# Gate and up products of SwiGLU feature tiles 4 to 7 by Strassen's seven products, with sums of input blocks and the residual parked in DRAM

## The chip, the cores and the metric

The kernel runs as one program on one core of a Trainium2 chip. The metric is the device time of one execution in microseconds (us), lower is better; the time of a kernel is the median of its runs. The result must agree with the reference in float32.

## The reference

A hybrid decoder trunk of two layers on 512 tokens of width 1024. Each layer is a half-step SwiGLU, a mixing of three kinds of attention, and a second half-step SwiGLU, each with an RMSNorm in front and behind. What the change touches is the SwiGLU, which runs four times:

```python
D_MODEL = 1024; SEQ = 512; DEPTH = 2
D_FF = ((8 * D_MODEL // 3 + 127) // 128) * 128        # 2816, 22 tiles of 128

def _swiglu(t, w_gate, w_up, w_down):
    return (jax.nn.silu(t @ w_gate) * (t @ w_up)) @ w_down
...
    h = x
    for l in range(DEPTH):
        f = _swiglu(_rmsnorm(h, ffn1_pre_g[l]), ffn1_w_gate[l], ffn1_w_up[l], ffn1_w_down[l])
        h = h + 0.5 * _rmsnorm(f, ffn1_post_g[l])
        u = _rmsnorm(h, mix_pre_g[l])
        ...                                           # three attentions of u, gated and merged
        h = h + _rmsnorm(merged @ w_out[l], mix_post_g[l])
        f = _swiglu(_rmsnorm(h, ffn2_pre_g[l]), ffn2_w_gate[l], ffn2_w_up[l], ffn2_w_down[l])
        h = h + 0.5 * _rmsnorm(f, ffn2_post_g[l])
    return h
```

All of it is float32. The names of tiles in the profile end in the sub-layer: a0 and c0 for the two SwiGLUs of layer 0, a1 and c1 for those of layer 1 (the views drop the digit, so that `pga` is a gate product of a0 or a1).

## The kernel before

**A float32 product is three matmuls.** Each operand is kept as a high and a low part, both in the type fp32r; `mm3` (L180 to L184) multiplies high by high, high by low and low by high into one PSUM bank. A split into the parts is a cast on ScalarE (L162) and a subtraction on VectorE (L163). The activations of a sub-layer lie transposed in two tiles `src.us`, each with four blocks of 128 of the model width by 512 tokens in two parts.

**Weights** come in units (class `Unit`, L209). A unit is fetched by one transfer of 512 KB, issued on SyncE (SP), into a ring "raw" of two buffers, and loaded by the split into the rings "wh" and "wl" of four buffers each (`BUFS`, L102). In the plain form a unit holds four blocks of 128 of the inner dimension by 256 columns, 128x1024 as the profile writes it.

**The order.** A queue `Q` (class `Queue`) holds jobs: a list of units and a generator that emits the matmuls. Before a job's matmuls the units of the next jobs are loaded until `AHEAD` = 4 units are ahead, and `fetch_ahead` fills the raw ring whenever a unit has given its buffer back. `weave` puts chains of other work (norms, attention, the end of a sub-layer) between the matmuls of the jobs by an estimate of PE time. When the program is built, a scheduler sets the order of each engine's queue out of this; on the chip each queue runs in order.

**One SwiGLU** (`ffn`, L548) goes through its 22 feature tiles in pairs. The first pair is a `halved` job: its matmuls are 256 tokens wide, so that it can start when half of the tokens are normalised. Each further pair has two plain jobs, `gates` and `ups`, of 48 matmuls each: 2 tiles x 8 blocks of the model width x 3, each 128x512 out of a 128x128 weight block. `hidden` takes Silu of the gate bank on ScalarE (L561) and multiplies by the up bank on VectorE (L566), for the first 16 tiles into the kept tiles `hr` in the rings "k" and "tri".

**The down projection** of the first 16 feature tiles goes in two chunks of 8 (`FC` = 8, `NC` = 2), and each chunk already by Strassen's seven products (`products`, `product`, L656): its first factor is a sum of blocks of `hr` (`first_factor`, L605, which splits it too), its second a sum of blocks of the down weights (class `BlockUnit`, L252), and the product is added into one of three pairs of PSUM accumulators. For every half of the inner blocks a `BlockUnit` keeps two weight blocks in tiles `bt`, which are fetched once and combined in place from product to product (L299 and the lines around it); products 3 and 4 fetch nothing into the raw ring:

```python
BLOCKS = ((0, 0), (1, 0), (0, 0), None, None, (0, 1), (1, 0))
```

Of a finished chunk one product follows after each further plain job. The last 6 feature tiles go through the plain `down` (L705), whose end is interleaved with the residual step, the norm and the transposition of each block of tokens into the next sub-layer's input (class `Sub`: `residual`, `normed`, `turned`).

**PSUM** has two rings of four banks: "mm" for gate and up products, "z" for the accumulators of the down products. **SBUF**: the residual stream `hT`, four tiles of 512 KB, stays in four of the eight buffers of the ring "o" through a SwiGLU. The mixing writes it to a DRAM tensor `hsave` at its start, uses the buffers for other things, and reads it back at its end.

Of the kernel before, what the change touches and what calls it, by code (L numbers as in the profile page):

```python
# [17 lines left out]
P = 128  # L18
# [4 lines left out]
def kernel(  # L23
# [50 lines left out]
    NF = 22  # L74
    FC = 8
    NC = 2
    TRI = (0, 512, 896, 1152)
    TRIW = 1280
    QLO = (0, 128, 256, 256)
# [24 lines left out]
    def stile(shape, tag, name, dt=F32R):  # L104
        return sb.tile(shape, dt, tag=tag, bufs=BUFS[tag], name=name)
# [4 lines left out]
    def pbank(tag, name):  # L110
        return ps.tile([P, S], F32, tag=tag, bufs=4, name=name)
# [97 lines left out]
    class Unit:  # L209
# [8 lines left out]

            return self.raw is None and self.h is None

        def ring(self):

            return True

        def fetch(self):
            if not self.waits():
# [25 lines left out]
    class BlockUnit(Unit):  # L252
# [13 lines left out]
        def waits(self):  # L266
            return not self.fetched

        def ring(self):
            return self.BLOCKS[self.n] is not None  # L270

        def block(self, dst, b):
            r = (b[0] * self.rows + self.k0) * P
# [3 lines left out]
        def fetch(self):  # L277
            if self.fetched:
                return
            self.fetched = True  # L280
            if self.n == 2:
                self.block(self.keep.get(0, self.k0), (0, 1))
            if self.n == 3:
                self.block(self.keep.get(1, self.k0), (1, 1))
            if self.ring():
                Q.fetched += 1
                self.raw = stile([P, self.nk, self.ncol], "raw", "raw_" + self.name, F32)
                self.block(self.raw[:], self.BLOCKS[self.n])

        def load(self):  # L290
            if self.h is not None:
                return
            self.fetch()
            t = self.keep.get(0, self.k0) if self.n >= 2 else None
            b = self.keep.get(1, self.k0) if self.n >= 3 else None
            if self.n < 2:
                src = self.raw[:]
            elif self.n == 2:
                nc.vector.tensor_tensor(t, t, self.raw[:], ALU.subtract)  # L299
                src = t  # L300
            elif self.n == 3:
                nc.vector.tensor_tensor(t, b, t, ALU.subtract)
                src = t
            elif self.n == 4:
                src = b
            elif self.n == 5:
                nc.vector.tensor_tensor(b, b, self.raw[:], ALU.subtract)
                src = b
            else:
                nc.vector.tensor_tensor(t, t, self.raw[:], ALU.subtract)  # L310
                src = t
            self.split_from(src)
            if self.ring():
                self.raw = None
                Q.fetched -= 1
            Q.fetch_ahead()

    class Keep:
# [14 lines left out]
    class Queue:  # L333
# [127 lines left out]
    class Sub:  # L461
# [54 lines left out]
        def normed(self, t):  # L516
# [31 lines left out]
    def ffn(l, src, wg, wu, wd, dst, name, spare, aside=None):  # L548
# [47 lines left out]
        def down_out(t, hf, pt):  # L596
# [5 lines left out]
            nc.vector.tensor_tensor(s[:], f, pt[:], ALU.add)  # L602
            return s[:]

        def first_factor(ci, n):  # L605
# [49 lines left out]

        def products(ci):  # L656

            def make(i, k0):

                if ci == 0:  # L660
                    return stile([P, 2, S], "qo"[i], f"bt{name}_{i}_{k0}", F32)[:]
                if k0 == 0:
                    st["bt", i] = stile([P, 2, 2, S], "k", f"bt{name}_{i}", F32)
                return st["bt", i][:, k0 // 2]
# [6 lines left out]
        marks, todo = {}, iter(())  # L671
        for f in range(0, NF, 2):
            ug = wpair(wg[l], ND, f * P, f"g{name}_{f}")
            uu = wpair(wu[l], ND, f * P, f"u{name}_{f}")
            if f == 0:
                marks["early"] = ug + uu
                for un, place in zip(ug + uu, ("tri", "tri", (spare, spare), (spare, spare))):
                    un.tags = place
                Q.add(ug + uu, lambda ug=ug, uu=uu: halved(0, ug, uu, 0), src.ready((0, 1)))
                Q.add([], lambda ug=ug, uu=uu: halved(0, ug, uu, 1), src.ready(range(NT)))  # L680
                marks["first"] = len(Q.jobs)
                continue
            ci = f // FC if f % FC == FC - 2 and f < NC * FC else None
            Q.add(ug, lambda f=f, ug=ug: gates(f, ug))
            for one in todo:
                Q.add(*one)
                break
            if ci is not None:
                Q.add([], lambda ci=ci: iter(first_factor(ci, 0) or ()))
            Q.add(uu, lambda f=f, uu=uu: ups(f, uu))  # L690
            if ci is not None:
                todo = products(ci)
            for one in todo:
                Q.add(*one)
                break
            if f == FC - 2 and name == "a0":
                Q.add([], vectors)
        if aside is not None:
            Q.add([], aside)
        f0 = NC * FC  # L700
# [322 lines left out]
    def mixing(l, src, ks, vs, dst):  # L1023
# [95 lines left out]
        def reload():  # L1119
            dst.begin()  # L1120
            new_h(f"m{l}")
            for i in range(NT):
                nc.sync.dma_start(hT[i][:], hsave[i])
# [62 lines left out]
    def begin():  # L1186

        sub = subs[0]
        new_h("x")
        Q.hold = True  # L1190
        nc.sync.dma_start(hT[0][:], x[0, 0:P, :])
        sub.gains()
        nc.sync.dma_start(hT[1][:], x[0, P:2 * P, :])
        Q.fetch_ahead()
        for t in range(2, NT):
            nc.sync.dma_start(hT[t][:], x[0, t * P:(t + 1) * P, :])
        sub.begin()
        for t in range(2):
            sub.squared(hT[t][:], sub.sh[t], 0, sub.fs[t][:])
            sub.normed(t)  # L1200
        for t in range(2):
            sub.turned(t)
            Q.jobs[0][0][t].load()
        for t in range(2, NT):
            sub.squared(hT[t][:], sub.sh[t], 0, sub.fs[t][:])
            yield ("wait", 2.0)
            sub.normed(t)
            yield ("wait", 3.0)
            sub.turned(t)
            yield ("pe", 0.9)  # L1210
# [49 lines left out]
```

## Time and profile before

| | |
|---|---|
| Time, median of 3 runs | 2494.75 us (2494.07 to 2495.52) |
| Profiled execution, its time | 2493.26 us |
| Its span | 2491.5 us |
| Mean granted TensorE clock | 0.997 |
| PE busy | 2449.6 us in 12178 recorded matmuls |
| VectorE (DVE) busy | 1541.3 us |
| ScalarE (ACT) busy | 1146.2 us |
| DMA | 270.54 MB, 109 GB/s on average |

The span runs from the first to the last event that the profiler recorded, so the execution's own time is a little longer. The page's rows read: line, engine, operation, tile written <- tiles read, shape, count, then busy time and mean duration in ns, then the idle time of the engine before these instructions and what ended it. PE is TensorE's matmul side, PEld its weight loads, SPq the queue that issues the transfers. Matmuls overlap in the pipeline: a matmul's duration is longer than the distance between two starts, and that distance is what a row of matmuls costs.

### The profile page before, as it was taken

The page shows a single profiled execution, that of the slowest core. Times are in us where ns is not written, and L with a number is a line of the kernel's source. Part 1 is how long each engine was busy: PE and PEld are TensorE (multiplying, and loading weights), DVE is VectorE, ACT ScalarE, POOL GpSimd, SP SyncE. Part 2 cuts the span into 40 slices and gives each one's busy share as a digit, 9 for nine tenths or more (in the row PEclk, how much of TensorE's full clock was granted, in tenths as well). Part 3 has the DMA queues.
Part 4 walks back from the last instruction along what each step waited for, and adds up shares of the span by engine and source line. Part 5 has one row for each costly group of instructions (what it writes and reads, how often), then busy time and mean ns, then how long its engine had stood idle before and what let it go on. Part 6 is the DMA issues. An engine that isn't in the chain of part 4 may idle for free.

```text
span 2491.5 us, 30949 instructions
## 1 busy us (share of the span) xinstructions
PE 2449.6 (98%) x12178; PEld 2065.6 (83%) x12178; DVE 1541.3 (62%) x2249; ACT 1146.2 (46%) x1873; POOL 76.3 (3%) x126
## 2 busy tenths in 40 slices
PE   8999999999999999999999999999999999999998
PEld 7888888888888788888888888888888888888887
DVE  4364667888676543556644546768787765435465
ACT  4333365666555433333433333546665554333333
POOL 0000000000110000000000000000001200000000
PEclk9999999999999999999999999999999999999999
DMA  5343334222222523433423333432222224233332
GB/s 178 102 136 119 114 131 144 60 77 76 69 77 80 183 83 104 134 120 96 157 88 113 122 129 116 140 115 76 77 60 85 78 97 155 88 109 126 127 101 102
DMA packets 235346, 270.54 MB, mean 109 GB/s; under 512 B 10408, under 2 KB 190656, under 8 KB 235200
## 3 DMA queue, kind: packets, MB, share of 16 engines
q1 hardware_dynamic: 235104, 268.53, 33.6%
q8 instruction: 95, 1.56, 0.3%
q14 instruction: 51, 0.42, 0.1%
q0 software_dynamic: 96, 0.03, 0.0%
HBM read 262.24 MB, written 6.29 MB: 108 GB/s over the span
## 4 chain that ended last, share of the span: by engine, by line
PE 83%; DVE 8%; ACT 5%; DMA 3%; issue 1%; SPq 0%; DVEq 0%; ACTq 0%
PE pgc L183 3%; PE pgc L182 3%; PE pgc L184 3%; PE puc L183 3%; PE puc L184 3%; PE puc L182 3%; PE pga L183 3%; PE pga L182 3%; PE pga L184 3%; PE pua L183 3%; PE pua L184 3%; PE pua L182 3%; PE pg L182 3%; PE pg L183 3%; PE pg L184 3%; PE pdc L183 2%
## 5 line engine op out<-in xcount | busy, mean ns | idle before, releaser
L182 PE MATMUL pg<-us_a,wh_wg 128*128 128x512 f32 x384 | 151.2, 394 | 0.0
L184 PE MATMUL pg<-us_a,wl_wg 128*128 128x512 f32 x384 | 149.8, 390 | 0.0
L183 PE MATMUL pg<-us_a,wh_wg 128*128 128x512 f32 x384 | 149.5, 389 | 0.0
L182 PE MATMUL puc<-us_b,wh_uc 128*128 128x512 f32 (+1 forms) x384 | 142.6, 372 | 2.1 <-DVE fb L492 2.1
L183 PE MATMUL puc<-us_b,wh_uc 128*128 128x512 f32 (+1 forms) x384 | 142.4, 371 | 0.0
L184 PE MATMUL puc<-us_b,wl_uc 128*128 128x512 f32 (+1 forms) x384 | 142.4, 371 | 0.0
L182 PE MATMUL pgc<-us_b,wh_gc 128*128 128x512 f32 x320 | 124.5, 389 | 0.0
L183 PE MATMUL pgc<-us_b,wh_gc 128*128 128x512 f32 x320 | 124.5, 389 | 0.0
L184 PE MATMUL pgc<-us_b,wl_gc 128*128 128x512 f32 x320 | 124.5, 389 | 0.0
L163 DVE TENSOR_TENSOR wl_uc<-raw_uc,wh_uc 128x1024 fp32r<-128x1024 f32 x44 | 53.9, 1225 | 104.5 <-ACT wh_uc L162 104.5
L163 DVE TENSOR_TENSOR wl_ua<-raw_ua,wh_ua 128x1024 fp32r<-128x1024 f32 x44 | 53.9, 1225 | 96.3 <-ACT wh_ua L162 96.2
L163 DVE TENSOR_TENSOR wl_ga<-raw_ga,wh_ga 128x1024 fp32r<-128x1024 f32 x40 | 49.0, 1225 | 65.8 <-ACT wh_ga L162 65.7
L162 ACT CAST wh_uc<-raw_uc 128x1024 fp32r<-128x1024 f32 x44 | 46.4, 1054 | 91.3 <-PE pgc L183 39.4
L163 DVE TENSOR_TENSOR wl_gc<-raw_gc,wh_gc 128x1024 fp32r<-128x1024 f32 x40 | 49.0, 1225 | 63.3 <-ACT wh_gc L162 63.3
L184 PE MATMUL pda<-wh_da,ala 128*128 128x512 f32 x224 | 87.1, 389 | 0.0
L182 PE MATMUL pda<-wh_da,aha 128*128 128x512 f32 x224 | 87.1, 389 | 0.0
L183 PE MATMUL pda<-wl_da,aha 128*128 128x512 f32 x224 | 87.1, 389 | 0.0
L182 PE MATMUL pdc<-wh_dc,ahc 128*128 128x512 f32 x224 | 87.1, 389 | 0.0
L183 PE MATMUL pdc<-wl_dc,ahc 128*128 128x512 f32 x224 | 87.1, 389 | 0.0
L184 PE MATMUL pdc<-wh_dc,alc 128*128 128x512 f32 x224 | 87.1, 389 | 0.0
L162 ACT CAST wh_ua<-raw_ua 128x1024 fp32r<-128x1024 f32 x44 | 46.3, 1053 | 85.2 <-PE pga L183 35.8
L184 PEld LDWEIGHTS pg<-us_a,wl_wg 128*128 128x128 f32 x384 | 72.1, 188 | 15.3
(435 smaller groups left out, 7282.5 us busy)
## 6 DMA issues: line engine op xcount, KB each, us to landing
raw_da<-in_ffn_w_down_dram SPq DMA_DIRECT2D x52, 512.0 KB, 3.3
raw_dc<-in_ffn_w_down_dram SPq DMA_DIRECT2D x52, 512.0 KB, 3.3
raw_wg<-in_w_gate_dram SPq DMA_DIRECT2D x48, 512.0 KB, 3.5
raw_ga<-in_ffn_w_gate_dram SPq DMA_DIRECT2D x44, 512.0 KB, 3.6
raw_ua<-in_ffn_w_up_dram SPq DMA_DIRECT2D x44, 512.0 KB, 3.7
raw_gc<-in_ffn_w_gate_dram SPq DMA_DIRECT2D x44, 512.0 KB, 3.6
raw_uc<-in_ffn_w_up_dram SPq DMA_DIRECT2D x44, 512.0 KB, 3.6
bta<-in_ffn_w_down_dram SPq DMA_DIRECT2D x16, 512.0 KB, 4.4
```

The source lines that it names most:

```text
L162: nc.scalar.copy(h_ap, src)
L163: nc.vector.tensor_tensor(l_ap, src, h_ap.bitcast(F32), ALU.subtract)
L182: nc.tensor.matmul(pt, lh, rh, start=start, stop=False, skip_group_check=free)
L183: nc.tensor.matmul(pt, lh, rl, start=False, stop=False, skip_group_check=free)
L184: nc.tensor.matmul(pt, ll, rh, start=False, stop=stop, skip_group_check=free)
```

## The change

Feature tiles 4 to 7 form a 4 x 4 group: `QF` = 4 tiles of features by 512 tokens. Gate and up product of this group no longer go tile by tile but as a 2 x 2 block product by Strassen's seven products, in halves of the features (2 tiles), of the model width (4 blocks) and of the tokens (256).

- `sums` forms four sums of blocks of the normalised input out of its high and low parts, 16 VectorE operations and 8 splits, in a job between the halved one and the second plain pair. The results lie in rings that are idle at this time ("o", "q", "v", "rs").
- `SumUnit` is a weight unit of one product: seven for each matrix, each 128x1024 like a plain one, of which four are sums or differences of blocks formed by one VectorE operation in a staging tile. 18 transfers of 512 KB bring what 16 brought before.
- `quad` emits one product, 4 blocks x 2 tiles x 3 = 24 matmuls of 256 columns, into one of three banks of the ring "mm", and then copies, adds, multiplies or takes Silu of what has become final. `ORDER` interleaves gate and up products: g0 to g5, u0, g6, u1 to u6 (its entry None adds no job). The first down product of chunk 0 follows; in the built order its first four matmuls stand between u5 and u6.
- A `BlockUnit` keeps one block instead of two: product 4 fetches the second block into the raw ring, and product 5 fetches two at once, into both raw buffers (`need`). `Queue.fetch_ahead` counts with `need`.
- The residual is parked in `hsave` during every SwiGLU: `normed` writes each block of tokens there as it goes by (in the first SwiGLU nothing is written, since the input x is the residual). `reload` brings it back, one tile in front of each of the plain jobs of tiles 16 to 19 in the program's text. The mixing no longer writes `hsave` itself.

In the built program PE has 12486 matmuls and other operations in place of 11911, VectorE 2388 in place of 2212, and SP issues 617 transfers in place of 517. (The profile's own counts differ a little.) The transfers for the reload are placed by the scheduler of the build earlier than in the text, in SP's queue ahead of the transfers of the later down units.

```diff
+    QF = 4
...
-        BLOCKS = ((0, 0), (1, 0), (0, 0), None, None, (0, 1), (1, 0))
+        BLOCKS = ((0, 0), (1, 0), (0, 0), (1, 1), (1, 1), (1, 1), (1, 0))
...
+        def need(self):
+            return 2 if self.n == 5 else 1
...
             self.fetched = True
+            Q.fetched += self.need()
             if self.n == 2:
-                self.block(self.keep.get(0, self.k0), (0, 1))
-            if self.n == 3:
-                self.block(self.keep.get(1, self.k0), (1, 1))
...
+                self.block(self.keep.get(self.k0), (0, 1))
+            self.raw, self.raw2 = (stile([P, self.nk, self.ncol], "raw", f"raw{i}_" + self.name, F32)
+                                   if i < self.need() else None for i in range(2))
+            self.block(self.raw[:], self.BLOCKS[self.n])
+            if self.raw2 is not None:
+                self.block(self.raw2[:], (0, 1))
...
+            src = r = self.raw[:]
+            if self.n in (2, 3, 6):
+                src = t = self.keep.get(self.k0)
+                a, b = (r, t) if self.n == 3 else (t, r)
+                nc.vector.tensor_tensor(t, a, b, ALU.subtract)
             elif self.n == 5:
+                nc.vector.tensor_tensor(r, r, self.raw2[:], ALU.subtract)
             self.split_from(src)
...
+    class SumUnit(Unit):
+        RING = ((0, 0), (0, 1), (1, 1), (0, 0), (0, 1), (1, 0), (1, 1))
...
+        def fetch(self):
+            if not self.waits():
+                return
+            Q.fetched += self.need()
+            if self.n in (2, 5):
+                self.keep[self.n] = stile([P, self.nk, self.ncol], "o", "s_" + self.name, F32)
+                self.block(self.keep[self.n][:], (1, 0) if self.n == 2 else (0, 0), 0, self.nk)
+            self.raw = stile([P, self.nk, self.ncol], "raw", "raw_" + self.name, F32)
+            self.block(self.raw[:], self.RING[self.n], 0, self.nk)
+
+        def load(self):
...
+            if self.n in (2, 3, 4, 5):
+                src = t = self.keep[5 if self.n == 5 else 2][:]
+                a, b, op = {2: (t, r, ALU.add), 3: (t, r, ALU.subtract), 4: (r, t, ALU.subtract),
+                            5: (t, r, ALU.subtract)}[self.n]
+                nc.vector.tensor_tensor(t, a, b, op)
+            self.split_from(src)
...
-                        if un.ring() and self.fetched == BUFS["raw"]:
+                        if self.fetched + un.need() > BUFS["raw"]:
...
+    def load_h(t, src=None):
+        nc.sync.dma_start(hT[t][:], hsave[t] if src is None else src[t * P:(t + 1) * P, :])
...
+        def normed(self, t, save=True):
...
+            if save:
+                nc.sync.dma_start(hsave[t], hT[t][:])
...
+        def sums():
+            places = (("o", "o"), ("o", "o"), ("q", "q"), ("v", "rs"))
...
+            for k in range(0, ND // 2, 2):
...
+                tt(b01[:], b(0, 1, 0), b(0, 1, 1), ALU.add)
+                tt(t[:], b01[:], b(0, 0, 0), sub)
+                tt(t[:], t[:], b(0, 0, 1), sub)
+                out(0, t[:])
...
+        def quad(f, up, n, un):
+            key = ("m", f, up, SUM[n])
+            if n in (0, 1, 2):
+                st[key] = pbank("mm", ...)[:].rearrange("p (m q) -> p m q", m=2)
...
+            for k in range(ND // 2):
+                for m in range(2):
+                    c = slice(m * P, (m + 1) * P)
+                    mm3(pt[:, m], un.h[:, k, c], un.l[:, k, c], bh[:, k], bl[:, k], opens and k == 0 and m == 0,
+                        ends and k == ND // 2 - 1, free=True)
+                    yield 3 * S // 2 * PE_US
...
+            if n in (0, 2, 3):
+                nc.scalar.copy(c, pt)
+                return
+            if n == 6:
+                c = pt
+            else:
+                nc.vector.tensor_tensor(c, c, pt, add)
+            if up:
+                nc.vector.tensor_tensor(r, r, c, mult)
+            else:
+                nc.scalar.activation(r, c, AF.Silu)
...
+        Q.add([], sums)
+        for job in plain(2)[2:]:
+            Q.add(*job)
...
+        ORDER = [(0, n) for n in range(6)] + [(1, 0), (0, 6)] + [(1, n) for n in range(1, 6)] + [None, (1, 6)]
...
+        for at, job in enumerate(quads(4)):
+            if at == 10:
+                Q.add([], lambda: iter(first_factor(0, 0) or ()))
+            if job is not None:
+                Q.add(*job)
...
+        for i, f in enumerate(range(NC * FC, NF, 2)):
+            for e, job in enumerate(plain(f)[2:]):
+                if 2 * i + e < NT:
+                    Q.add([], lambda t=2 * i + e: reload(t))
+                Q.add(*job)
+                Q.add(*next(down1))
...
         def run():
             Q.until(marks["first"])
-            for i in range(NT):
-                nc.sync.dma_start(hsave[i], hT[i][:])
```

More of the change, by code (lines that the diff above doesn't have):

```diff
@@ L267, in waits, with need @@
             return not self.fetched
-        def ring(self):
-            return self.BLOCKS[self.n] is not None
+        def need(self):
+            return 2 if self.n == 5 else 1
         def block(self, dst, b):
@@ L293, in load @@
             self.fetch()
[L294 to L305, printed above, removed]
-            elif self.n == 5:
[L307 to L311, printed above, removed]
@@ new lines, in load, with __init__, block @@
+            self.raw = None
+            Q.fetched -= self.need()
+            Q.fetch_ahead()
+    class SumUnit(Unit):
+        RING = ((0, 0), (0, 1), (1, 1), (0, 0), (0, 1), (1, 0), (1, 1))
+        def __init__(self, n, src, c0, keep, name):
+            super().__init__(src, 0, ND // 2, c0, QF // 2 * P, name, -1.0 if n == 6 else None)
+            self.n, self.keep = n, keep
+        def block(self, dst, b, k, nk):
+            r, c = (b[1] * self.nk + k) * P, self.c0 + b[0] * self.ncol
+            nc.sync.dma_start(dst, self.src[r:r + nk * P, c:c + self.ncol].rearrange("(k p) c -> p k c", p=P))
+        def fetch(self):
[8 more added lines that the diff above has]
+        def load(self):
+            if self.h is not None:
+                return
+            self.fetch()
+            src = r = self.raw[:]
+            if self.n in (2, 3, 4, 5):
[4 more added lines that the diff above has]
+            self.split_from(src)
+            self.raw = None
+            Q.fetched -= 1
@@ L603, in down_out @@
             return s[:]
+        def sums():
+            places = (("o", "o"), ("o", "o"), ("q", "q"), ("v", "rs"))
+            ts = [[stile([P, ND // 2, S // 2], g, f"t{name}_{i}_{x}") for x, g in enumerate(p)]
+                  for i, p in enumerate(places)]
+            st["t"] = ts
+            tt, sub = nc.vector.tensor_tensor, ALU.subtract
+            for k in range(0, ND // 2, 2):
+                ks = slice(k, k + 2)
+                b = lambda i, j, part: src.us[i][:, ks, part, HALVES[j]].bitcast(F32)
+                b01, t, w = (sb.tile([P, 2, S // 2], F32, tag="f32t", bufs=5, name=f"{x}{name}_{k}") for x in ("b01", "t", "w"))
+                out = lambda i, v: split(ts[i][0][:, ks], ts[i][1][:, ks], v)
+                tt(b01[:], b(0, 1, 0), b(0, 1, 1), ALU.add)
+                tt(t[:], b01[:], b(0, 0, 0), sub)
+                tt(t[:], t[:], b(0, 0, 1), sub)
+                out(0, t[:])
+                tt(w[:], b(1, 1, 0), b(1, 1, 1), ALU.add)
+                tt(t[:], w[:], t[:], sub)
+                out(1, t[:])
+                tt(w[:], w[:], b01[:], sub)
+                out(2, w[:])
+                tt(t[:], t[:], b(1, 0, 0), sub)
+                tt(t[:], t[:], b(1, 0, 1), sub)
+                out(3, t[:])
+                yield 0.0
@@ L605, in first_factor @@
+        QTO = ((0, 0), (0, 0), (1, 1), (0, 1), (0, 1), (1, 1), (1, 0))
         def first_factor(ci, n):
@@ L669, in products, with plain @@
                 yield uns, (lambda n=n, uns=uns: product(ci, n, uns))
-        marks, todo = {}, iter(())
-        for f in range(0, NF, 2):
+        marks = {}
+        def plain(f):
             ug = wpair(wg[l], ND, f * P, f"g{name}_{f}")
             uu = wpair(wu[l], ND, f * P, f"u{name}_{f}")
[L675 to L697, printed above, removed]
@@ new lines, in plain @@
+            return ug, uu, (ug, lambda: gates(f, ug)), (uu, lambda: ups(f, uu))
+        ug, uu, _, _ = plain(0)
+        marks["early"] = ug + uu
+        for un, place in zip(ug + uu, ("tri", "tri", (spare, spare), (spare, spare))):
+            un.tags = place
+        Q.add(ug + uu, lambda: halved(0, ug, uu, 0), src.ready((0, 1)))
+        Q.add([], lambda: halved(0, ug, uu, 1), src.ready(range(NT)))
+        marks["first"] = len(Q.jobs)
+        Q.add([], sums)
+        for job in plain(2)[2:]:
+            Q.add(*job)
@@ new lines, in ffn, with quads @@
+        if name == "a0":
+            Q.add([], vectors)
+        ORDER = [(0, n) for n in range(6)] + [(1, 0), (0, 6)] + [(1, n) for n in range(1, 6)] + [None, (1, 6)]
+        def quads(f):
+            keeps = {}, {}
+            for one in ORDER:
+                if one is None:
+                    yield None
+                    continue
+                up, n = one
+                un = SumUnit(n, (wg, wu)[up][l], f * P, keeps[up], f"{'gu'[up]}{name}_{f}_{n}")
+                yield [un], lambda up=up, n=n, un=un: quad(f, up, n, un)
@@ new lines, in ffn @@
+        down0, down1 = products(0), products(1)
+        for at, job in enumerate(quads(4)):
[3 more added lines that the diff above has]
+                Q.add(*job)
+        Q.add(*next(down0))
+        for f in range(2 * QF, NC * FC, 2):
+            for e, job in enumerate(plain(f)[2:]):
+                if f == NC * FC - 2 and e == 1:
+                    Q.add([], lambda: iter(first_factor(1, 0) or ()))
+                Q.add(*job)
+                for one in down0:
+                    Q.add(*one)
+                    break
@@ L698, in ffn, with reload @@
+        Q.add(*next(down1))
+        def reload(t):
+            if t == 0:
+                new_h("r" + name)
+            load_h(t, x[0] if name == "a0" else None)
+            return iter(())
+        for i, f in enumerate(range(NC * FC, NF, 2)):
+            for e, job in enumerate(plain(f)[2:]):
+                if 2 * i + e < NT:
+                    Q.add([], lambda t=2 * i + e: reload(t))
+                Q.add(*job)
+                Q.add(*next(down1))
         if aside is not None:
@@ L1122, in reload @@
             for i in range(NT):
-                nc.sync.dma_start(hT[i][:], hsave[i])
+                load_h(i)
         down(w_out[l], ND, lambda k, c=FULL: list_act(st["ms"])(k, c), lambda t, hf, pt: pt[:], f"wo{l}", dst, marks, reload)
@@ L1199, in begin @@
             sub.squared(hT[t][:], sub.sh[t], 0, sub.fs[t][:])
-            sub.normed(t)
+            sub.normed(t, False)
         for t in range(2):
@@ L1206, in begin @@
             yield ("wait", 2.0)
-            sub.normed(t)
+            sub.normed(t, False)
             yield ("wait", 3.0)
```

36 lines of the change are left out of this document (22 added, 14 removed).

## The prediction

> **What bounds the kernel now.** I read the page first: shares, slices, then the chain that ended last.
>
> ```profile
> span 2491.5 us, 30949 instructions
> PE 2449.6 (98%) x12178; PEld 2065.6 (83%) x12178; DVE 1541.3 (62%) x2249; ACT 1146.2 (46%) x1873; POOL 76.3 (3%) x126
> PE   8999999999999999999999999999999999999998
> PEclk9999999999999999999999999999999999999999
> PE 83%; DVE 8%; ACT 5%; DMA 3%; issue 1%; SPq 0%; DVEq 0%; ACTq 0%
> ```
>
> TensorE is busy for 98% of the span at the full granted clock, and the chain lies on it for 83%. The profiled execution took 2493.26 us, 1.76 us more than its span; the median of the runs, 2494.75, is 1.5 us above it. Time can go only where matmuls go, and a wait anywhere else costs only once it reaches TensorE. So I cut out the stage that the change rewrites: gate and up products of feature tiles 4 to 7 of the first feed-forward, in the view by windows (columns: length, then busy time of PE, PEld, DVE and ACT with counts, clock, DMA share, GB/s).
>
> ```profile
> 64.79:108.31 43.52, 43.52 (x194) 36.04 (x193) 13.71 (x13) 11.58 (x14) 1.09 (x2) 1.00 0.31 98
> 53.91:64.79 10.88, 10.88 (x50) 9.01 (x49) 3.14 (x3) 2.60 (x4) 0.00 (x0) 1.00 0.31 96
> ```
>
> PE has no gap in it; VectorE works 13.7 of 43.5 us. One plain job (48 matmuls of 512 columns) takes 10.88 us, so one matmul takes 0.2267 us. The new products move 256 columns at a time, which the halved first job already does; its timeline:
>
> ```profile
> 32.08 0.28 PE L184 MATMUL pga<-us_x,w_ga 128*128 128x256 f32 x1
> 34.24 0.28 PE L184 MATMUL pga<-us_x,w_ga 128*128 128x256 f32 x1
> ```
>
> Between these starts lie 18 matmuls: 0.120 us each, more than half of 0.2267. (The 0.28 us of a row is a matmul's latency: from the next start to its own end 0.16.) Strassen's eighth is partly eaten by that.
>
> **The matmuls.** Per feed-forward 4 tiles x 2 matrices x 8 k x 3 = 192 matmuls of 512 columns go: 43.52 us. In come 14 products x 4 k x 2 x 3 = 336 of 256 columns: 336 x 0.120 = 40.32 us, 2.88 us a product. That is -3.20 us per feed-forward, -12.8 us for the four, if PE never waits. A rule speaks against even this. The Trainium skill, "TensorE: Matmul & The Clock Gate", section "Back-to-back issue gap", gives sustained spacings of about 81 ns at 128 columns and 131 ns at 512; a line between them puts 256 columns at 98 ns, an estimate, 0.75 of the wide one, where the rows here say 0.53.
>
> **What feeds them.** Each product has a weight unit of its own (128x1024), where before 8 units did. VectorE and ScalarE prices:
>
> ```profile
> L163 DVE TENSOR_TENSOR wl_ua<-raw_ua,wh_ua 128x1024 fp32r<-128x1024 f32 x44 | 53.9, 1225 | 96.3 <-ACT wh_ua L162 96.2
> L299 DVE TENSOR_TENSOR bta<-bta,raw_da 128x1024 f32<-128x1024 f32 x8 | 9.8, 1224 | 3.4 <-DMA raw_da<-in_ffn_w_down_dram 3.4
> L566 DVE TENSOR_TENSOR hra<-pua,sa 128x512 f32<-128x512 f32 x32 | 22.1, 692 | 55.9 <-PE pua L184 55.9
> L162 ACT CAST wh_ua<-raw_ua 128x1024 fp32r<-128x1024 f32 x44 | 46.3, 1053 | 85.2 <-PE pga L183 35.8 <-PE pua L183 33.0 <-DMA raw_ua<-in_ffn_w_up_dram 13.4
> L652 ACT COPY fa<-pda 128x512 f32<-128x512 f32 x16 | 9.3, 582 | 5.0 <-PE pda L184 5.0
> ```
>
> VectorE in the stage: 14 splits and 8 block sums at 1.22, 6 adds and 4 multiplies at 0.69: 33.8 us, with the first down factor 35, of 40.3. It stays under PE, but not by much, and its queue is in order. ScalarE has 14 x 1.05 + 10 x 0.59 = 20.6 us. So the question is lateness, not sums. The chain of waits shows at a boundary what one of the two raw buffers costs per turn:
>
> ```profile
> 1209.65 1.06 ACT wh_dc L162
> 1210.74 1.24 DVE wl_dc L163
> 1211.99 3.81 DMA raw_ga<-in_ffn_w_gate_dram
> 1215.83 1.07 ACT w_ga L162
> ```
>
> Cast 1.09, split 1.25, transfer 3.8: 6.15 us, 3.1 us per unit with two buffers, against 2.88 us of PE. Only the four units split ahead, and the block sums, which free a buffer before the split, keep this level. I follow it by hand with these prices and 0.16 us for the last matmul to end, in the built program's order of each queue. Time 0 is the first quad product; g and u are gate and up products, d the first down product's units; columns: block sum done, cast done, split done, needed by PE.
>
> ```
> g4   5.6   6.6   8.4  11.5      u3  23.0  24.0  25.3  28.8
> g5   6.7   7.8   9.6  14.4      u4  26.4  27.5  29.7  31.7
> u0    -   10.4  11.7  17.3      u5  27.9  29.0  30.9  34.6
> g6    -   12.8  14.1  20.2      u6    -   31.3  32.7  37.4
> u1    -   16.7  18.0  23.0      d0    -   33.0  34.3  37.4
> u2  19.1  20.2  21.5  25.9      d0'   -   37.8  39.1  41.4
> ```
>
> No unit is late. The thin places are accumulators: g4 waits for a copy that stands behind u0's cast (11.0 against 11.5), g6 for an add behind u2's block sum (19.7 against 20.2), u4 for a copy behind u6's cast (31.9 against 31.7). The worst is u6: it reuses the bank that u5's add must read first; only four down matmuls (0.9 us) stand between, and that add is queued on VectorE behind the split of d0', whose transfer leaves at 32.7 behind two reloads of the residual and lands at 36.7. Split at 39.1, add done at 39.75; PE is there at 38.55. Price 1.2 us per feed-forward, 4.8 in all; bounds 0.2 (an add of 0.69 against the cover of 0.9, and hand-over) and 3 (the transfer at the 4.9 of a reload, and one more in its way):
>
> ```profile
> raw_ga<-in_ffn_w_gate_dram SPq DMA_DIRECT2D x44, 512.0 KB, 3.6
> raw_da<-in_ffn_w_down_dram SPq DMA_DIRECT2D x52, 512.0 KB, 3.3
> hm<-hsave SPq DMA_DIRECT2D x8, 512.0 KB, 4.9
> hsave<-hx SPq DMA_DIRECT2D x4, 512.0 KB, 3.1
> ```
>
> Sums of the input: 16 adds and 8 splits of 512 columns, 24 x 0.69 = 16.6 us of VectorE under the 21.8 us of the second plain pair, where it has twice 3.14 us of other work; its results are read only at the third product, 5.8 us later. Price 0, up to 2 if PE's bank copies queue behind it.
>
> Down blocks: product 4 now fetches a block that was kept, and product 5 two, which fill both buffers. From product 4's end: second raw lands at 0.6, sum 1.8, split 4.7; the next pair lands at 8.2, sum 9.4, split 11.75 (needed 13.6); the up units after it 15.25 (16.3) and 17.6 (19.0). Margin 1.1 us; eight places; I take 1 in all, 0 to 6. In the first feed-forward one such place also has the memory's squares and their table loads on ScalarE ahead of a cast:
>
> ```profile
> 313.00 1.28 ACT L561
> 315.84 1.28 ACT L774
> 319.34 1.28 ACT L561
> ```
>
> Three loads and a square put the cast at 10.5 and the following up unit at 17 against 16.3: 1 us, 0 to 3.
>
> Parking: the writes at the attention's start were there before (hsave<-hx); they move into the norm step, and three more boundaries get four each. On SP they wait for the residual of their tile, with weight units of the second plain pair behind them, which PE needs 20 us later: 0, from -1 to 2. The 16 reloads are priced above, with d0'. The four early block transfers in the first 25 us go, where PE's slice shows 8: 0, down to -1.
>
> Sum: -12.8 + 4.8 + 1 + 1 = -6.0 on the profiled 2493.26: 2487.3; on the median of the runs, 2488.7. With all low bounds -12.8 + 0.8 - 2 = -14; with the high ones of the quads and the down products -12.8 + 12 + 6 + 3 = +8.
>
> **Rivals.**
> *Transfers slow down (slower).* Between g6 and u6 four landings stand one behind the other: u1, u3, u6, d0'. The stage has 18 weight transfers, four reloads and two kept down blocks in 40 us, 24 x 0.524 MB = 12.6 MB, 312 GB/s if none came early, where the stage before moves 98. The start shows what is to be had:
>
> ```profile
> 2.00:10.00 8.00, 1.94 (x8) 1.57 (x8) 2.47 (x9) 3.51 (x10) 1.18 (x4) 1.00 0.98 325
> ```
>
> Landings of 4.8 instead of 3.8 add 4 us per feed-forward: 4 x 5.2 + 2 - 12.8 = +10, 2505. It decides from about 0.5 us more per landing, where the 3.2 us are gone. For it: that rate. Against: four transfers are issued ahead of the stage, so about 260 GB/s remain, and two pairs rarely overlap. The Trainium skill, "DMA: Bandwidth & Descriptors", section "Latency and other measured facts", puts memory latency at 0.2 us on average and 2 us under high load; by that, as an estimate, landings could grow by 1.8 us, beyond this rival's price. Chance 0.20.
>
> *The margins close (no change).* Half of that, or VectorE's in-order queue later by half a microsecond at each thin place: 3 us per feed-forward, 12 + 2 - 12.8 = +1, 2496. For it: 35 of 40 us on VectorE; against: the table has 4 us of slack for nearly all units. Chance 0.16.
>
> *Narrow matmuls are worse than half.* If weight loads set the pace at 0.75 of the wide pitch, 336 x 0.170 = 57.1 us, +13.6 per feed-forward, +54: 2549. The rows of the halved job speak against it. By the skill's "Back-to-back issue gap" this is the outcome; the trace's 0.120 disagrees. Chance 0.02.
>
> **How the numbers follow.** Chance of the forecast 0.62, its own range 2482 to 2495. I call 0.2% (5 us) what a measurement of this kernel can tell from no change: below 2489.8 faster, above 2499.7 slower. The forecast gives 0.50 faster and 0.12 same; the closed margins 0.02 faster, 0.12 same, 0.02 slower; slow transfers and narrow matmuls 0.22 slower. Together 0.52, 0.24, 0.24. The range takes the forecast's low end, 2482, and reaches into the slow transfers: 2503.
>
> **What would show it.** In the new profile: quad matmuls at a pitch of 0.120 (right) or more (narrow rival); the stage from the first g0 to the last u6 some 41 to 42 us, with PE's largest wait in it before u6, released by the add of u5's accumulator, about 1 us, behind a split of a down unit; block and unit landings near 3.8 us (4.3 and above: the slow rival). Waits of PE elsewhere in the feed-forward under 1 us each. The prediction is wrong if waits in the quads sum to over 3 us per feed-forward, or if the second plain pair waits for the sums.

## The result, and the profile after

| | before | after |
|---|---|---|
| median, 8 runs each | 2494.41 us | 2504.4 us (2502.56 to 2510.86) |
| ratio | | 1.0044, 95% interval 1.0033 to 1.0055 |
| profiled execution, its span | 2493.26, 2491.5 | 2502.56, 2500.8 |

The kernel became slower by 10 us, where 6 us less were forecast; the profiled executions differ by 9.3. The page of the changed kernel, in the rows that were read before:

```profile
span 2500.8 us, 32630 instructions
PE 2440.8 (98%) x12754; PEld 2082.6 (83%) x12754; DVE 1680.8 (67%) x2425; ACT 1200.1 (48%) x1953; POOL 76.3 (3%) x126
PE 75%; DVE 10%; DMA 6%; ACT 6%; issue 2%; ACTq 0%; DVEq 0%; SPq 0%
```

PE is busy 8.8 us less although it runs 576 more recorded matmuls, and the chain that ended last lies on it for 75% instead of 83%; VectorE and DMA took most of what it lost. The view by windows from the first quad product to the last, in a0, c0, a1 and c1 (length, then busy PE, PEld, DVE, ACT, POOL, granted clock, DMA share, GB/s):

```profile
64.97:109.60 44.63, 42.11 (x341) 41.18 (x341) 31.74 (x32) 21.02 (x27) 0.00 (x0) 1.00 0.68 224
944.28:988.75 44.47, 41.92 (x342) 41.07 (x341) 32.21 (x32) 20.74 (x25) 0.00 (x0) 1.00 0.69 225
1307.35:1354.04 46.69, 43.09 (x341) 42.16 (x340) 32.19 (x32) 20.73 (x25) 0.00 (x0) 0.97 0.66 219
2186.93:2232.60 45.67, 43.48 (x342) 42.58 (x341) 32.16 (x32) 20.74 (x25) 0.00 (x0) 0.96 0.69 226
```

Each window holds four down matmuls of 0.2267 us, 0.91 together. Without them and the forecast 40.32 us of matmuls there remain 3.40, 3.24, 5.46 and 4.44 us, 16.5 in all, where 4.8 were forecast. Gaps between starts of matmuls make up 13.9 of it: 7.3 before u6, 2.8 before g6, 2.6 before u4, and about 1.2 in the first matmul behind each wait, 0.10 us each time. The other 2.7 lie almost all in the last two windows, where the granted clock was 0.97 and 0.96. DMA moves 224 GB/s where the stage before moved 98.

Where the waits are, in the waits of PE over the whole changed kernel (in all, times, longest), those of the last down matmuls of c0 (`pdc`) among them:

```profile
PE mt L926 <- DVE fa L758: 3.9, 2, 2.6
PE puc L183 <- DVE cc L700: 3.3, 2, 2.0
PE pua L183 <- DVE ca L700: 3.3, 2, 1.9
PE pga L183 <- DVE hra L700: 2.1, 2, 1.5
...
PE pdc L183 <- DVE fc L635: 1.3, 1, 1.3
PE puc L183 <- ACT cc L695: 1.3, 1, 1.3
...
PE pdc L184 <- DVE wl_dc L164: 1.2, 2, 0.8
...
PE pua L183 <- ACT ca L695: 0.7, 2, 0.5
```

The same two places outside the quads in the kernel before:

```profile
PE pdc L183 <- DVE wl_dc L163: 0.5, 1, 0.5
...
PE pdc L182 <- ACT wh_dc L162: 0.2, 1, 0.2
...
PE mt L786 <- DVE fa L654: 0.2, 1, 0.2
```

The rows of `mt` and `pdc` lie outside the quads: the transposes of the memory wait for a bank that an add of the down products must read first, and so does the first row of the late down matmuls; the second is a weight split that comes late. Together they are 3.9 and 2.5 us, where the kernel before has 0.2 and 0.7. All the other rows shown have one form: PE waits for an operation that empties a PSUM bank, on VectorE (before u6 and g6) or on ScalarE (`cc` and `ca` of L695, before u4). What held that operation back is seen in VectorE's timeline before u6 in a0, with the PE rows around the wait:

```profile
103.92 0.28 PE L184 MATMUL pua<-ta,wh_ua 128*128 128x256 f32 x1
104.04 0.28 PE L185 MATMUL pua<-ta,wl_ua 128*128 128x256 f32 x1
104.85 0.40 PE L183 MATMUL pda<-wh_da,aha 128*128 128x512 f32 x1
106.64 0.39 PE L183 MATMUL pua<-ta,wh_ua 128*128 128x256 f32 x1 [1.39 <-DVE ca L700]
...
104.76 1.23 DVE L164 TENSOR_TENSOR wl_da<-raw_da,wh_da 128x1024 fp32r<-128x1024 f32 x1 [1.80 <-ACT wh_da L163]
105.91 0.68 DVE L700 TENSOR_TENSOR ca<-ca,pua 128x512 f32<-128x512 f32 x1
```

u5 ended at 104.3, VectorE was idle for 1.80 us until 104.76, and yet u5's add ran at 105.91 only: it stands in the queue behind the split of d0' (`wl_da`), which waited for ScalarE's cast and that for a transfer. The order was forecast, and the pitch too (103.92 to 104.04 is 0.12 us). The amount was not.

### The profile page after: what moved, and what is told of

Read it like the earlier page. It is cut to its first block, busy times and chain, and to the rows that moved or that the text cites. A ratio compares the mean times of both kernels' runs of the same rounds, so it can differ in the third digit from the quotient of the medians.

```text
span 2500.8 us, 32630 instructions
## 1 busy us (share of the span) xinstructions
PE 2440.8 (98%) x12754; PEld 2082.6 (83%) x12754; DVE 1680.8 (67%) x2425; ACT 1200.1 (48%) x1953; POOL 76.3 (3%) x126
## 4 chain that ended last, share of the span: by engine, by line
PE 75%; DVE 10%; DMA 6%; ACT 6%; issue 2%; ACTq 0%; DVEq 0%; SPq 0%
PE pg L183 3%; PE pg L184 3%; PE pg L185 3%; PE pga L184 3%; PE pga L183 3%; PE pga L185 3%; PE puc L183 3%; PE puc L184 3%; PE pua L183 3%; PE puc L185 3%; PE pua L184 3%; PE pua L185 3%; PE pgc L183 2%; PE pgc L184 2%; PE pgc L185 2%; PE pda L184 2%
## 5 line engine op out<-in xcount | busy, mean ns | idle before, releaser
L183 PE MATMUL puc<-us_b,wh_uc 128*128 128x512 f32 (+1 forms) x368 | 131.5, 358 | 3.4 <-DVE fb L526 2.1
L184 PE MATMUL puc<-us_b,wh_uc 128*128 128x512 f32 (+1 forms) x368 | 131.1, 357 | 0.0
L185 PE MATMUL puc<-us_b,wl_uc 128*128 128x512 f32 (+1 forms) x368 | 131.1, 357 | 0.0
L184 PE MATMUL pgc<-us_b,wh_gc 128*128 128x512 f32 (+1 forms) x304 | 113.2, 372 | 0.0
L183 PE MATMUL pgc<-us_b,wh_gc 128*128 128x512 f32 (+1 forms) x304 | 113.2, 372 | 0.0
L185 PE MATMUL pgc<-us_b,wl_gc 128*128 128x512 f32 (+1 forms) x304 | 113.2, 372 | 0.0
L164 DVE TENSOR_TENSOR wl_da<-raw_da,wh_da 128x1024 fp32r<-128x1024 f32 x44 | 53.8, 1222 | 52.8 <-ACT wh_da L163 52.7
L164 DVE TENSOR_TENSOR wl_dc<-raw_dc,wh_dc 128x1024 fp32r<-128x1024 f32 x44 | 53.8, 1223 | 51.4 <-ACT wh_dc L163 51.3
L183 PEld LDWEIGHTS pg<-us_a,wh_wg 128*128 128x128 f32 x384 | 72.2, 188 | 14.3
L184 PEld LDWEIGHTS pg<-us_a,wh_wg 128*128 128x128 f32 x384 | 72.1, 188 | 14.3
```

Source lines behind the costliest of these rows:

```text
L164: nc.vector.tensor_tensor(l_ap, src, h_ap.bitcast(F32), ALU.subtract)
L183: nc.tensor.matmul(pt, lh, rh, start=start, stop=False, skip_group_check=free)
L184: nc.tensor.matmul(pt, lh, rl, start=False, stop=False, skip_group_check=free)
L185: nc.tensor.matmul(pt, ll, rh, start=False, stop=stop, skip_group_check=free)
```

## The experiments

Theory T: the new transfers slow the landings of the units beside them. Theory Q: the order of the queues, with little work between a product and the next on its bank, costs the time whatever lands. Theory D: what is lost outside the quads comes from the doubled raw transfers of the down products. Each kernel was run beside the kernel before, in three rounds, so kernels of different rounds are compared by their ratios. In the table "quads" is the time from the start of the first to the start of the last quad matmul without the 512-column ones, the sum of four; without any wait it would be 4 x 335 x 0.120 = 160.8 us.

| kernel | median us | ratio to before (95%) | quads us |
|---|---|---|---|
| changed kernel | 2504.4 | 1.0044 (1.0033 to 1.0055) | 177.4 |
| late reloads | 2501.62 | 1.0028 (1.0019 to 1.0037) | 172.1 |
| late reloads, late kept blocks | 2497.49 | 1.0012 (1.0003 to 1.0021) | 169.4 |
| the same, with cover | 2490.6 | 0.9986 (0.9977 to 0.9994) | 162.9 |
| cover alone | 2495.57 | 1.0008 (0.9999 to 1.0017) | 166.4 |
| two kept blocks | 2505.25 | 1.0037 (1.0024 to 1.005) | 181.9 |
| cover, late reloads, two kept blocks | 2486.68 | 0.9973 (0.9962 to 0.9984) | 168.4 |
| the same, late kept blocks | 2481.39 | 0.9955 (0.994 to 0.9969) | 162.6 |
| two covers alone | 2500.69 | 1.003 (1.0018 to 1.0042) | 177.6 |

**Late reloads.** The transfer is pinned behind what SP was given before it:

```diff
-            load_h(t, x[0] if name == "a0" else None)
+            tc.keep_in_program_order(load_h(t, x[0] if name == "a0" else None))
```

> The changed kernel with the four reloads of the residual issued where the text has them (tiles 16 to 19), so that none lands during the quad products. Theory T (transfers): the added transfers stretch the landings of the units beside them (4.4 to 6.6 us where the plain stage has 3.5); without reloads the second unit of the first down product lands 0.8 to 1.5 us earlier, the split that stands before u5's add goes earlier by as much, and the wait before u6 (1.56, 1.43, 2.08, 2.21 us in the four feed-forwards) falls to about 0.5; the waits before g6 and u4 stay. About -4 us against the changed kernel. Theory Q (order): the add stands behind that split in VectorE's queue whatever lands beside it; the waits stay within 0.3 us each, -1 us or less. Theory D (down refetch): the rest of the loss lies at the ends of the feed-forwards and is not touched.

The quads are 5.3 us shorter and the ratio is lower by 0.0016, 4 us, with intervals that overlap a little. Half of the 5.3 is the clock, which was 1.00 in all four windows here; the waits became 2.6 us shorter. The waits before u6, counted by starts, fell from 1.56, 1.43, 2.08 and 2.21 us to 0.90, 0.56, 0.82 and 1.15. Those before g6 stayed in sum (2.8 us), those before u4 rose from 2.6 to 3.8. The fall of 3.9 us before u6 is as T said, though a little more was left there than 0.5 us each, and 1.1 us came back before u4.

**Late kept blocks too.**

```diff
             if self.n == 2:
-                self.block(self.keep.get(self.k0), (0, 1))
+                b = self.block(self.keep.get(self.k0), (0, 1))
+                if self.keep.first:                      # chunk 0
+                    tc.keep_in_program_order(b)
```

> As the run with late reloads, and the two kept blocks of the first down chunk are also fetched where the text has them, after the quad products. T: the unit of u1 lands in 3.8 instead of 4.4 to 5.6 us, the split before g5's add goes 1 us earlier, and the waits before g6 and u4 (together 1.46, 1.45, 2.02, 0.45 us) fall to 0.3 or less; the quad stage comes to 41 to 42 us without its four down matmuls; -8 us against the changed kernel, near the kernel before. Q: another -1 us at most, the stage stays at 43 us.

The kernel is another 4 us faster, 2.7 of it in the quads. The DMA view by issues (KB each, us to landing), for issues from 73 to 77 us of a0, of the changed kernel and then of this one:

```profile
bta<-in_ffn_w_down_dram SPq DMA_DIRECT2D x2, 512.0 KB, 5.6
raw_ua<-in_ffn_w_up_dram SPq DMA_DIRECT2D x1, 512.0 KB, 5.6
...
raw_ua<-in_ffn_w_up_dram SPq DMA_DIRECT2D x1, 512.0 KB, 3.8
```

u1's unit lands in 3.8 us instead of 5.6, and the wait before g6 in a0 is gone (under 0.2 us). In a0 the quads took 41.7 us. But 8.6 us remain over the four (169.4 - 160.8), mostly as waits before u4 (3.0) and u6 (4.0), though the landings are now nearly those of the forecast's table: T alone falls short.

**With cover.** The first down product goes whole between u5 and u6, and the split of its next first factor behind u6:

```diff
-            if job is not None:
-                Q.add(*job)
-        Q.add(*next(down0))
+            Q.add(*(next(down0) if job is None else job))
+        Q.add([], lambda: iter(first_factor(0, 1) or ()))
...
-            if n < 6:
+            if n < 6 and (ci, n) != (0, 0):
                 first_factor(ci, n + 1)
```

> As the run with late reloads and late kept blocks, and the whole first down product (24 matmuls of 512 columns, 5.4 us) stands between u5 and u6 instead of four of its matmuls. Q: this takes away the wait before u6, 5 to 7 us over the four feed-forwards, whatever the transfers do. T: that wait is mostly gone already in the run without cover, so 0 to -2 us against it.

-6.9 us, as Q said, and faster than the kernel before. The wait before u6, 4.0 us, is gone; those before u4 fell too, from 3.0 to 1.2 us, which Q had not said, and what the moved split has in that was not tried apart. The quads are 2.1 us from the sum without waits. In a0 the window, which now holds 24 matmuls of 512 columns (5.44 us), has PE without a gap:

```profile
64.40:110.28 45.88, 45.88 (x361) 44.93 (x361) 33.08 (x33) 23.66 (x31) 0.00 (x0) 1.00 0.54 161
```

45.88 - 5.44 = 40.44 us; VectorE's 33 us hold nothing up.

**Cover alone**, with the transfers as in the changed kernel:

> The changed kernel with the whole first down product between u5 and u6 and the transfers as they are. If order alone is what cost the time (Q), the wait before u6 goes and with it 7 us, 2497. If the transfers set it (T), the second unit of the first down product is as late as before (its split ends 41.0 us after the first quad product, and PE wants it at 40.1), so the wait moves in front of the down product's second half, about 1 us per feed-forward, and the waits before g6 and u4 stay: -3 us, 2501.

2495.57, a little below Q's 2497. The wait before u6 is gone and none took its place in the down product; those before g6 and u4 stay. T's forecast for this run was wrong. With cover, taking the transfers away lowers the ratio from 1.0008 to 0.9986, 5.5 us; without it from 1.0044 to 1.0012, 8 us: both causes are real, and their sizes nearly add.

**Two kept blocks**: `BlockUnit` and the tiles `bt` as in the kernel before.

> The changed kernel with the down blocks as before: two kept blocks for each half, products 3 and 4 without a transfer into the raw ring, product 5 with one. Theory D: the waits that are new outside the quad products (2.5 and 1.5 us in front of the memory's transposes, 2.4 us in the last down matmuls of the second feed-forward) come from the doubled raw transfers of the down products, which leave the two raw buffers late at the end; they go, -5 to -6 us against the changed kernel, and the quad products stay as they are or lose up to 1 us each, because four kept blocks and not two are fetched near them. If the parked residual's writes or the reloads are behind these waits, nothing changes there.

The time did not move measurably, where 5 to 6 us less were expected, and still the mechanism of D holds: the wait of `mt` is gone, and those of `pdc` are down from 2.5 to 0.9 us. What they had cost was given back in the quads, 4.5 us longer, where the waits before u6 rose to 3.06, 2.90, 2.15 and 2.68 us. The issues between 97.9 and 98.3 us of this kernel, 33.9 us after its first quad product, and the one between 98.5 and 99.3 of the changed kernel, at 34.1, are the same unit, d0':

```profile
raw_da<-in_ffn_w_down_dram SPq DMA_DIRECT2D x1, 512.0 KB, 6.0
...
raw_da<-in_ffn_w_down_dram SPq DMA_DIRECT2D x1, 512.0 KB, 4.5
```

With late reloads it took 3.9 us. So landings of 3.9, 4.5 and 6.0 go with waits before u6 of 0.90, 1.56 and 3.06 us: what the landing loses, PE loses. Why the reloads beside it and d0' landed later here than in the changed kernel, from almost the same issue times, is not settled.

**Cover, late reloads and two kept blocks.**

> The cover between u5 and u6, the reloads where the text has them, and the two kept down blocks of before (which in this order are fetched behind the quad products, because one of the two rings that hold them is busy until then). If the waits of the quad products and those of the doubled raw pairs add up as the single runs say, the quads keep the 40.3 to 41.1 us of the run with cover, and the waits before the memory's transposes (2.2 and 2.9 us) and in the last down matmuls of the second feed-forward (2.4 us) go: 2490.6 - 7 = 2484, 0.996 of the kernel before. If the four kept blocks collide with the quad units again, as in the run with two kept blocks alone, the waits come back before g8's or d1's matmuls and the time stays at 2490.

2486.68: the waits outside went, but against the run with cover and late transfers the quads lost 5.5 us, mostly before g6 (1.48 us in a0, 1.83 in c1) and not where the expectation put it. Two kept blocks are again issued among the quad units; the issues from 73 to 77 us:

```profile
bta<-in_ffn_w_down_dram SPq DMA_DIRECT2D x2, 512.0 KB, 6.1
raw_ua<-in_ffn_w_up_dram SPq DMA_DIRECT2D x1, 512.0 KB, 6.2
```

**The same, with late kept blocks.**

> As the run with cover, late reloads and two kept blocks, and the kept blocks of the first down chunk are fetched where the text has them, behind the quad products. In that run two of them were issued between the units of g6 and u1 and landed in 6.0 and 6.3 us, u1's unit beside them in 6.2, and the wait before g6 was 1.48 us in the first feed-forward. T: without them u1's unit lands in 3.9, the wait before g6 falls to 0.3 or less, the quad products come to 40.3 to 41.1 us each, together 163 instead of 168.4: 2486.7 - 5 = 2481.5. If the wait before g6 has another cause, 2486.

2481.39 against 2481.5 expected, 0.9955 of the kernel before. Its four windows, from a0 to c1, each with 5.44 us of down matmuls:

```profile
65.00:110.88 45.88, 45.88 (x361) 44.92 (x361) 32.96 (x33) 23.56 (x31) 0.00 (x0) 1.00 0.54 161
938.09:984.60 46.51, 46.30 (x362) 44.93 (x361) 33.32 (x33) 23.16 (x29) 0.00 (x0) 1.00 0.54 159
1296.97:1343.07 46.10, 46.10 (x361) 44.92 (x360) 33.32 (x33) 23.67 (x29) 0.00 (x0) 1.00 0.54 160
2169.19:2215.58 46.39, 46.28 (x361) 44.91 (x360) 33.41 (x33) 23.11 (x29) 0.00 (x0) 1.00 0.54 159
```

DMA moves 160 GB/s here instead of 224, and the idle time of PE is 0.3 us in all; counted by starts, the quads are 1.8 us from the sum without waits. The profiled execution took 2481.43 us, 11.8 less than before; the matmuls alone were to give 12.8.

**Two covers alone**: the run with cover alone, and u1 ahead of g6.

```diff
-        ORDER = [(0, n) for n in range(6)] + [(1, 0), (0, 6)] + [(1, n) for n in range(1, 6)] + [None, (1, 6)]
+        ORDER = [(0, n) for n in range(6)] + [(1, 0), (1, 1), (0, 6)] + [(1, n) for n in range(2, 6)] + [None, (1, 6)]
```

> The changed kernel with its transfers as they are, the whole first down product between u5 and u6, and u1 moved ahead of g6, so that two products and not one stand between g5 and g6. Q: a wait of PE for a bank is bought off by work placed between, whatever the transfers do: the waits before g6 (1.01, 0.74, 0.44, 0.37 us with the one cover) go to zero, -2.5 us against the run with one cover, 2493. T: the same units are as late as before, and the next product to need one waits instead, u2 or u4: 0 to -1 us, 2495.

Both were wrong: 5 us slower. The wait before g6 went, and u5 now waits 1.61, 3.61, 1.17 and 3.51 us; about 4 us more of the quads' time are the clock, 0.93 and 0.97 in the windows of c0 and c1. ScalarE's timeline in c0, the PE row that waits, the DMA row of the transfer that ends ScalarE's idle time, and the row of the waits of PE for the whole kernel:

```profile
979.70 1.04 ACT L163 CAST wh_dc<-raw_dc 128x1024 fp32r<-128x1024 f32 x1 [3.76 <-DMA raw_dc<-in_ffn_w_down_dram]
980.65 0.58 ACT L695 COPY cc<-puc 128x512 f32<-128x512 f32 x1
...
981.28 0.58 PE L183 MATMUL puc<-tc,wh_uc 128*128 128x256 f32 x1 [3.46 <-ACT cc L695]
...
raw_dc<-in_ffn_w_down_dram SPq DMA_DIRECT2D x1, 512.0 KB, 6.6
...
PE puc L183 <- ACT cc L695: 8.0, 4, 3.5
```

The build's scheduler put the copy of u3's bank behind the cast of d0', and d0' landed in 6.6 us beside two reloads. The queue is ScalarE's this time. Neither theory alone foretells such a case; a late landing and a bank's reader queued behind it do.

## Why the prediction was wrong

**The matmuls: right.** -3.20 us per feed-forward at a pitch of 0.12 us. In the kernels whose waits are gone, a0 shows 40.4 us for the stage. By the Trainium skill, "TensorE: Matmul & The Clock Gate", section "Back-to-back issue gap", 256 columns would cost 0.75 of 512, an estimate; the runs disagree, with 0.120 of 0.2267 us, 0.53.

**The waits in the quads: the step that failed.** The price was 4.8 us, and 16.5 were measured. The place that was named, u6, took 7.3 us, and its mechanism was the forecast one; g6 and u4, priced at nothing, took 5.4, and the rest is the matmuls behind each wait and the clock. The table gave every unit a landing of 3.8 us, and it left the two kept down blocks out: it counted them in the rival's rate, not in the queue. They were issued 8.3 and 9.4 us after the first quad product, among the units of g6 and u1, and u1's unit took 5.6 us. So the wait before g6 came (0.79, 0.07, 1.66 and 0.31 us), against a margin of 0.5 us in the table, and together with the wait before u4 it pushed d0' back by 1.4 us, whose own landing then took 4.5. The second fault was the thin places themselves. With landings as in the table, in the run with both late, 8.6 us of waits were left and not 4.8: u4's margin was already -0.2 in the table and was priced at nothing.

**The down blocks and the memory's norm: too small.** They were priced at 1 and 1 us. Near the place named for the memory's table loads an up unit comes late, and two starts of matmuls lie 0.4 us further apart than the pitch, no more. The doubled raw transfers delay the last units of the chunk, and with them the adds in front of the memory's transposes (3.9 us in two feed-forwards, 0.2 before) and c0's last down matmuls (2.5, 0.7 before). With two kept blocks this went, but for 0.2 us in c0.

**Sums and parking: right.** In a0, from the second plain pair's start to the first quad product 22.23 us passed, and 21.79 before, with PE busy throughout; the memory's vectors have moved into it. The written residual cost nothing that shows: the late down matmuls of c0 ran without the longer waits as soon as the raw pairs went, with the writes still there. One new wait does lie beside the writes, at the start of c0 and c1, before the transposes of a late block of tokens:

```profile
PE utb L565 <- DVE nhb L485: 2.6, 2, 1.3
```

It cost nothing against the kernel before: there the same transposes start 11.7 us after the first up unit is issued (890.98 to 902.71 in c0), and here too (892.12 to 903.90). In the kernel before a stretch of slow clock filled that time.

**The clock.** 2.7 us of the quads' loss lie in windows with a granted clock of 0.97 and 0.96. These are means: in the traces the clock is at 0.50 for 3.4 us at a time (twice that in a few places) and at 1.00 otherwise, as in these stretches of the changed kernel's last two quads:

```profile
1351.40:1354.80 3.40, 3.40 (x17) 3.30 (x16) 1.18 (x2) 0.64 (x1) 0.52 (x1) 0.50 0.71 247
2228.60:2232.10 3.50, 3.50 (x19) 3.50 (x18) 1.44 (x2) 0.49 (x1) 0.00 (x0) 0.51 0.67 186
```

The same four stages had 1.00 in the kernel before, which has such stretches elsewhere, at 894.6, 1253.0 and 2130.2 us. In the traces of all nine kernels with quads, such a stretch lies in a quad stage only beside a wait of PE of over 2 us: in six of the eight stages with such a wait, from 0.7 us before to 1.5 us after its end, and in none of the other 28. So a long wait seems to cost up to 1.7 us more (half of 3.4) in slow matmuls, an estimate; that the wait is the cause was not tried.

**The rivals.** Transfers that slow down were put at 2505 with a chance of 0.20, and the result is 2504.4, outside the range by 1.4 us. The mechanism is in part that rival's, and the closed margins stand beside it (2496 forecast, 2497.49 in the run without the transfers). The two were treated as exclusive, and they nearly add: a landing is late, and a thin place passes it on, as u6 does in full. That the number is so near 2505 is luck: the rival had 20.8 us in the quads and 2 outside, and 16.5 and 5.5 were measured. The sum: -12.8 + 16.5 + 5.5 outside the quads = 9.2 us, against 9.3 measured.

## What to carry to other kernels

When a faster product brings more transfers than the work it replaces, follow every transfer in the built order of its queue, those that are needed much later too: the scheduler of this build issued them well ahead of their place in the text, and they slowed the ones that were needed at once. Where an engine both splits arriving weights and empties accumulators in one queue, a late landing holds the accumulator back, so put a whole independent product between two uses of a bank and keep transfers without hurry out of the stage. A margin of half a microsecond in a table made with undisturbed durations is no margin.

## What was not expected of the hardware

In the quads of the changed kernel 79 transfers of 512 KB landed in 3.2 to 6.7 us. Counting those that overlap by more than 1 us: with at most one other beside it, mostly 3.4 to 3.8 us; with three or more beside it in its time, 4.2 to 6.7; and where three were under way at its issue already, 5.7 to 6.7. The DMA view of the changed kernel from 94 to 100 us, where two units and three reloads are issued:

```profile
DMA packets 1021, 1.89 MB, mean 315 GB/s; under 512 B 47, under 2 KB 559, under 8 KB 1021
hra<-in_x_dram SPq DMA_DIRECT2D x3, 512.0 KB, 5.7
raw_da<-in_ffn_w_down_dram SPq DMA_DIRECT2D x2, 512.0 KB, 4.5
```

A group seems to share a rate, so each further transfer of 0.524 MB delays the others by up to 0.524/0.315 = 1.7 us, an estimate from this row's mean. The Trainium skill, "DMA: Bandwidth & Descriptors", section "Specifications", gives about 358 GB/s as the HBM limit of one core. The 315 here lie below it, but the same kernel moved more at its start, 388 GB/s from 6 to 12 us:

```profile
DMA packets 1432, 2.33 MB, mean 388 GB/s; under 512 B 96, under 2 KB 1120, under 8 KB 1432
```
